# Attention in a decoder trunk: normalising the probabilities, or normalising their product with V

## The chip, the cores and the metric

The kernel runs on one core of a Trainium2 chip. The metric is the device time of one execution in microseconds (us). Before the change it is 1347.07 us, the median of three runs (1344.91, 1347.07, 1347.83).

## What is computed

A two-layer decoder trunk over 512 tokens of width 1024, in float32. Layer AB has a sparse mixer A (8 heads) and a forgetting mixer B (8 heads); layer C has a mixer of 16 heads with three branches: a compressed, a selected and a window branch, each scaled by a learned gate. After each mixer comes an output projection and a squared-ReLU MLP. Cut to what matters here:

```python
def masked_softmax(s, mask):
    s = jnp.where(mask, s.astype(jnp.float32), -jnp.inf)
    m = jnp.max(s, axis=-1, keepdims=True)
    m = jnp.where(jnp.isfinite(m), m, 0.0)
    e = jnp.where(mask, jnp.exp(s - m), 0.0)
    return e / jnp.maximum(jnp.sum(e, axis=-1, keepdims=True), 1e-30)
...
        p = masked_softmax(logits, causal[None, None]).astype(v.dtype)
        return jnp.einsum('bhqs,bshd->bqhd', p, v)
...
        out = gb[..., 0:1] * o_c + gb[..., 1:2] * o_s + gb[..., 2:3] * o_w
```

The division by the sum, and the gate, scale a whole row of `p`, one number for each query and head. So they can be applied to `p`, or to the row of `p @ v`.

## The kernel before

Activations lie feature by token (128 features x 512 tokens, a tile of 256 KB). Dense products take each operand as two fp32r parts, high and low, and three matmuls a product (`mm3`); weights arrive in tiles `raw`, and are split into `whi` and `wlo`. The results stand in PSUM tiles `psd` (`psn`, `psv`, `psva` for some).

The program is written as many small generators, and a planner (`Planner`, L134) puts their instructions in order when the program is built: at each step it takes the instruction that can start first by a table of costs and latencies. So the order on each engine is fixed at build time, and every engine runs its own list in that order. The generators share numbered slots: a generator that asks for a slot (`TU.get`, `PST.get`) waits in a line, first come first served, until one is put back. The profile gives all of these instructions one line, L299 (`group` and `Queue` record them), so its rows are told apart by the names of tiles.

Attention works on pairs of heads. A pair (in layer C, one branch of a pair) is eight units: two heads by four query blocks of 128, with 1 to 4 key blocks (128 to 512 columns). `unit` (L667) does one of them:

1. it takes one of the four SBUF slots `TU` (tile `t`) and one of two PSUM slots `PSS` (`pss`), and TensorE computes the scores;
2. VectorE adds the mask and finds the row's extremum `nm` in one custom instruction; ScalarE takes the exponential, with the row's sum `den` read from its accumulator;
3. VectorE takes the reciprocal `rec` of `den`, 128x1; GpSimd or VectorE, as the planner sees fit, multiplies `t` by `rec` and by the gate (1 in layer AB);
4. TensorE transposes `t` block by block into one of the two PSUM slots `PST` (`ptp`), after which `t` goes back to `TU`, and ScalarE or VectorE copies `ptp` to the pair's tile `pt`.

At most about six units of a pair are under way at once (`WIN`, L40). When all eight are done, `pv` (L689) multiplies `pt` with V into the only slot `PSO` (`po`): the two heads write the two halves of the 128 rows. In layer AB `o_evac` (L696) then splits `po` into `oh` and `ol`, the operands of the output projection. In layer C `pv_c` (L1529) adds three things in the same `po`: the selected branch, the window branch, and the compressed branch (one matmul, `vcb` by `ptc`), and then splits it. `pv_ab` (L1085) and `pv_c` call these.

While attention runs, TensorE also has dense products to do: in layer AB the last input projections and the half of the output projection whose heads are done (`half_out`, L1107); in layer C the query projections `q1` to `q7` of `ORDER_C` (L42) and again `half_out`. Behind the last pair stands `last_out` (L1136), which keeps the product with the last pair's `oh` back until nine other products (27 matmuls) are done.

Of the kernel before, what the change touches and what calls it, by code (L numbers as in the profile page):

```python
# [11 lines left out]
OP = mybir.AluOpType  # L12
# [119 lines left out]


class Planner:  # L134
    """Emits the instructions of many cooperating generators, each in its own order, always the one
    whose operands and engine are ready first; a generator yields an instruction, a choice of
    instructions, a slot it needs or a future it waits for."""

    def __init__(self, tc):
        self.free = {}  # L140
# [177 lines left out]
def trunk(ctx: ExitStack, tc: tile.TileContext, A):  # L318
# [36 lines left out]
    def small(n, name="sm"):  # L355
        return mp.tile([P, n], F32, tag=f"m{n}", name=name)

    def copy(out, src):
        return [SC.activation(out, src, AF.Copy), V.tensor_copy(out, src)]
# [30 lines left out]
    pev = C["pev"].rearrange("p (a b) -> p a b", b=8)  # L390
    w2k, w2v, fold = C["w2k"], C["w2v"], C["fold"]

# [1 line left out]
    jobs = []  # L394
    job_added = [Future()]

# [134 lines left out]
    def futures(n):  # L531
        return [Future() for _ in range(n)]

# [1 line left out]
    class Stats:  # L535
        def __init__(self, rows=P, total=KT, cols=S):
            self.rows, self.total, self.n, self.cols = rows, total, 0, cols
# [112 lines left out]
    def get2(slots, name, dtype=None):  # L650
        return (yield ("all", [slots.get(name, dtype), slots.get(name, dtype)]))

# [1 line left out]
    def scores(ps, qs, kk, qb):  # L654
        n = P * (qb + 1)
        q = qs[:, qb * P:(qb + 1) * P]
# [7 lines left out]
        return bass.AP(tensor=base.tensor, offset=base.offset,  # L664
                       ap=[base.ap[0], [S + P, qb + 1], [1, P]])

    def unit(qs, kk, qb, bias, pt, h, fut, gate=None):  # L667
        n = P * (qb + 1)
        t = yield TU.get("t")
        b = yield from bias(t)  # L670
        ps = yield PSS.get("pss")
        yield scores(ps, qs, kk, qb)
        nm, den, rec = small(1, "nm"), small(1, "den"), small(1, "rec")
        yield V.tensor_tensor_reduce(out=t[:, :n], in0=ps[:, :n], in1=b, op0=OP.add, op1=OP.min,
                                     scale=-0.125, scalar=3e38, accum_out=nm)
        put(PSS, ps)
        yield SC.activation(t[:, :n], t[:, :n], AF.Exp, scale=-1.0, bias=nm, accum_out=den)
        yield V.reciprocal(rec, den)
        g = 1.0 if gate is None else gate
        yield [e.tensor_scalar(t[:, :n], t[:, :n], rec, g, op0=OP.mult, op1=OP.mult) for e in (G, V)]  # L680
        tt = yield PST.get("ptp")
        yield group([T.transpose(tt[:, j * P:(j + 1) * P], t[:, kb * P:(kb + 1) * P], ident)
                     for kb in range(qb + 1) for j in [kb if h == 0 else qb - kb]])
        put(TU, t)
        yield copy(pt_dst(pt, h, qb), tt[:, :n].rearrange("p (a b) -> p a b", b=P))
        put(PST, tt)
        done(fut)
# [5 lines left out]
                                  pt[:, kb, kb * P:S] if h == 0 else pt[:, 4 - kb, 0:m],  # L693
                                  start=first and kb == 0, stop=last and kb == 3) for h in range(2)])

    def o_evac(ps, fut):  # L696
        oh, ol = yield from get2(O, "oh")
        yield copy(oh, ps)
        yield minus(ol, ps, f(oh))
        put(PSO, ps)  # L700
        done(fut, (oh, ol))

# [1 line left out]
    wab = A["wab"]  # L704
    x0 = futures(KT)
    u = futures(KT)
# [351 lines left out]
    def attention_ab():  # L1058
        for kind in ("b", "a"):
            for i in range(4):  # L1060
                q = yield qf[kind, i]
                k = yield kf[kind, i]
                pt = yield PT.get("pt")
                fs = []
                for n_ in range(8):
                    if kind == "b":
                        h, qb = n_ // 4, n_ % 4
                        if qb == 0:
                            yield cumf[2 * i + h]
                            bt = yield B.get("bb")  # L1070
                            yield SY.dma_start(bt, cumd[2 * i + h, :].partition_broadcast(P))
                            bb = [bt, 4]
                        bias = b_bias(bb, P * (qb + 1))
                    else:
                        h, qb = n_ % 2, n_ // 2
                        yield scf[qb]
                        bias = plain_bias(scr[qb])
                    fu = Future()
                    fs.append(fu)
                    spawn(unit(q[h], k[h], qb, bias, pt, h, fu), PR_ATT)  # L1080
                    if len(fs) > WIN:
                        yield fs[-WIN]
                spawn(pv_ab(kind, i, fs, pt, q, k), PR_PV)

    def pv_ab(kind, i, fs, pt, q, k):  # L1085
        for x in fs:
            yield x
        put(Q, *q)
        for x in k:
            put(K, *x)  # L1090
        if kind == "b":
            yield vbf[i // 2]
            v = vb
        else:
            yield vaf
            v = va
        po = yield PSO.get("po")
        yield from pv(po, pt, [[v[kb][:, (2 * i + h) * 64:(2 * i + h) * 64 + 64] for kb in range(4)]
                               for h in range(2)], True, True)
        put(PT, pt)  # L1100
        if i == 3:
            put(O, *v)
        yield from o_evac(po, och[(4 if kind == "b" else 0) + i])


# [1 line left out]
    def half_out(wo, half, och, base, spill, base_ready=None):  # L1107
        fs = futures(KT)
        for m in range(KT):
# [61 lines left out]
    ready = half_out(A["wout0"], 1, och, lambda m: A["xT"][:, m, :], spa)  # L1171
    st1, u1, hT = last_out(A["wout0"], 0, och, spa, ready, 1, "h1")

# [1 line left out]
    def mlp(hT, u, st, w1, w2, after, halves=False):  # L1175
        rnf, rbf = Future(), Future()
        spawn(layer_norm(st, rnf, rbf), PR_ATT)
# [71 lines left out]

    mlp(hT, u1, st1, A["w1"][0], A["w2"][0], after0)  # L1250

# [1 line left out]
    wc = A["wc"]  # L1253
    rnc, rbc, rotc = Future(), Future(), Future()
    spawn(layer_norm(st2, rnc, rbc, rotc), PR_ATT)
# [251 lines left out]
    def attention_c():  # L1507
        for pr in range(8):
            g = pr // 4
            q = yield qsc[pr]  # L1510
            po = Future()
            for bi, br in enumerate(("s", "w")):
                kk = (yield kst[br])[g]
                gat = yield gatf
                pt = yield PT.get("pt")
                fs = []
                for qb in range(4):
                    n = P * (qb + 1)
                    for h in range(2):
                        col = 3 * (2 * pr + h) + 1 + bi  # L1520
                        fu = Future()
                        fs.append(fu)
                        spawn(unit(q[h], kk, qb, plain_bias(cm[:, S - n:S]), pt, h, fu,
                                   gate=gat[:, qb, col:col + 1]), PR_ATT)
                        if len(fs) > WIN:
                            yield fs[-WIN]
                spawn(pv_c(pr, bi, fs, pt, q, po), PR_PV)

    def pv_c(pr, bi, fs, pt, q, pof):  # L1529
        g = pr // 4  # L1530
        for x in fs:
            yield x
        yield vsf
        if bi == 0:
            po = yield PSO.get("po")
        else:
            po = yield pof
        vv = [vsv[kb][:, 128 * bi + 64 * g:128 * bi + 64 * g + 64] for kb in range(4)]
        yield from pv(po, pt, [vv, vv], bi == 0, False)
        put(PT, pt)  # L1540
        if bi == 0:
            done(pof, po)
            return
        ptc = yield ptcf[pr // 2]
        vcb = yield vcf
        yield T.matmul(po, vcb[:, g, pr % 2, :], ptc, start=False, stop=True)
        if pr % 2:
            put(B, ptc)
            put(Q, *((yield qsc[pr - 1]) + q))
# [2 lines left out]
                put(K, *(yield kst[br])[g])  # L1552
        if pr == 7:
            put(O, *gbox["vsw"])
        yield from o_evac(po, occ[pr])

    spc = dram("spc")
    ready = half_out(A["wout1"], 0, occ, lambda m: spb[m], spc, spb_ready)
# [156 lines left out]
```

## Time and profile before

| | |
|---|---|
| median of three runs | 1347.07 us |
| span of the profiled execution, first to last instruction | 1347.5 us |
| TensorE (PE) busy | 1269.8 us, 94% |
| VectorE (DVE) busy | 830.8 us, 62% |
| ScalarE (ACT) busy | 632.3 us, 47% |
| GpSimd (POOL) busy | 450.0 us, 33% |

The profile lists no time around the span. The program stands in this order in the span: layer AB's input projections and attention to about 280 us, its output projection and MLP to about 677, layer C's projections from there, layer C's attention from about 745 to 945, its output projection, and the second MLP to the end. A matmul's row lasts until its result has drained, while the next one has already started; so the time that a matmul costs TensorE is read from the start of one to the start of the next.

### The profile page before, as it was taken

Reading aid. Unit: us, or ns where it says so; the run is one execution under the profiler, and the core shown is the slowest. Engines: PE = TensorE matmul, PEld = TensorE weight load, DVE = VectorE, ACT = ScalarE, POOL = GpSimd, SP = SyncE. Lnnn points to the kernel's source line nnn. Section 1 sums busy time; section 2 is a strip of 40 time slices with the busy share of each in tenths; the row PEclk is TensorE's granted clock in tenths of the full one; section 3 lists DMA queues with packets and bytes.
Section 4 is the critical chain, followed back from the end, with each engine's and each line's share of the span. In section 5 each row is a group of like instructions: output and inputs, shape, how many; then the busy total and the mean of one; then the engine's idle time right before and its main releaser. Section 6 shows DMA issues by size and latency. Waiting matters only on the chain.

```text
span 1347.5 us, 18599 instructions
## 1 busy us (share of the span) xinstructions
PE 1269.8 (94%) x6226; PEld 1011.4 (75%) x6226; DVE 830.8 (62%) x1709; ACT 632.3 (47%) x1331; POOL 450.0 (33%) x428
## 2 busy tenths in 40 slices
PE   6789998997999999999998899999989999999996
PEld 4668766675888888888877566666778888888896
DVE  6999977838434434345677877675644343443475
ACT  4465587742423424334345687776333242342442
POOL 3755887544300000000366656555440000000044
PEclk8899999998999999999997999999989999999998
DMA  6112212153232232232423200013523223232242
GB/s 227 65 55 72 87 63 70 64 193 97 94 99 97 94 101 95 96 100 99 161 66 119 101 24 17 9 35 123 170 74 101 94 98 98 95 102 94 95 155 96
DMA packets 71455, 127.80 MB, mean 95 GB/s; under 512 B 7928, under 2 KB 12536, under 8 KB 71360
## 3 DMA queue, kind: packets, MB, share of 16 engines
q1 hardware_dynamic: 71360, 126.62, 28.5%
q8 instruction: 50, 0.82, 0.3%
q14 instruction: 45, 0.37, 0.1%
HBM read 118.18 MB, written 8.40 MB: 94 GB/s over the span
## 4 chain that ended last, share of the span: by engine, by line
PE 75%; DVE 17%; issue 4%; ACT 2%; POOL 1%; DMA 0%; SPq 0%; POOLq 0%; DVEq 0%; ACTq 0%
PE psd L299 61%; PE po L299 4%; PE ptp L299 3%; PE pss L299 3%; DVE t L299 2%; DVE acc L299 2%; DVE scr L299 1%; DVE m L299 1%; DVE q L299 1%; PE psv L299 1%; DVE ul L299 1%; DVE wlo L299 1%; DVE hT L299 1%; PE pstat L299 1%; DVE whi L299 1%
## 5 line engine op out<-in xcount | busy, mean ns | idle before, releaser
L299 ACT ACTIVATE whi<-raw 128x512 fp32r<-128x512 f32 (+2 forms) x386 | 238.1, 619 | 473.6 <-PE psd L299 447.4
L299 POOL TENSOR_TENSOR wlo<-raw,whi 128x512 fp32r<-128x512 f32 (+1 forms) x143 | 193.2, 1354 | 730.7 <-ACT whi L299 422.7
L299 PE MATMUL psd<-uh,whi 128*128 128x512 f32 x760 | 305.9, 403 | 11.3 <-ACT uh L299 6.3
L299 PE MATMUL psd<-uh,wlo 128*128 128x512 f32 x760 | 301.5, 397 | 1.6 <-POOL wlo L299 1.6
L299 PE MATMUL psd<-ul,whi 128*128 128x512 f32 x760 | 301.3, 396 | 0.0
L299 DVE TENSOR_TENSOR wlo<-raw,whi 128x512 fp32r<-128x512 f32 (+1 forms) x253 | 183.4, 726 | 122.4 <-ACT whi L299 122.1
L299 PE MATMUL psd<-al,whi 128*128 128x512 f32 (+1 forms) x576 | 210.6, 366 | 0.0
L299 PE MATMUL psd<-ah,whi 128*128 128x512 f32 (+1 forms) x576 | 210.6, 366 | 0.0
L299 PE MATMUL psd<-ah,wlo 128*128 128x512 f32 (+1 forms) x576 | 210.5, 365 | 0.0
L299 PEld LDWEIGHTS psd<-uh,whi 128*128 128x128 f32 x760 | 146.3, 193 | 42.5 <-ACT uh L299 6.3
L299 PEld LDWEIGHTS psd<-uh,wlo 128*128 128x128 f32 x760 | 145.5, 191 | 34.3 <-POOL wlo L299 3.2
L299 PEld LDWEIGHTS psd<-ul,whi 128*128 128x128 f32 x760 | 146.1, 192 | 28.5 <-DVE ul L299 0.5
L299 ACT ACTIVATE t<-t,nm 128x128 f32<-128x128 f32 (+2 forms) x192 | 107.2, 559 | 46.0 <-DVE nm L299 43.1
L299 DVE TENSOR_TENSOR hT<-psd,hT 128x512 f32<-128x512 f32 (+1 forms) x88 | 56.3, 641 | 109.8 <-PE psd L299 109.8
L299 PEld LDWEIGHTS psd<-al,whi 128*128 128x128 f32 x576 | 108.6, 189 | 17.6 <-DVE al L299 0.2
L299 PEld LDWEIGHTS psd<-ah,whi 128*128 128x128 f32 x576 | 108.6, 189 | 17.6
L299 PEld LDWEIGHTS psd<-ah,wlo 128*128 128x128 f32 x576 | 108.6, 189 | 17.5
L299 DVE SCALAR_TENSOR_TENSOR t<-psd,rb 128x512 f32<-128x512 f32 x64 | 44.1, 691 | 108.3 <-PE psd L299 108.3
L299 PEld LDWEIGHTS ptp<-call,t 128*128 128x128 f32 x480 | 57.1, 141 | 54.9 <-POOL t L299 17.4
L299 PE MATMUL ptp<-call,t 128*128 128x128 f32 x480 | 83.4, 279 | 13.3 <-DVE t L299 9.5
L299 POOL TENSOR_SCALAR t<-t,rec,gat 128x128 f32<-128x128 f32 (+3 forms) x103 | 65.4, 639 | 64.1 <-DVE rec L299 48.3
L299 ACT ACTIVATE pt<-ptp 128x384 f32<-128x384 f32 (+3 forms) x186 | 77.6, 434 | 19.2 <-PE ptp L299 18.0
(245 smaller groups left out, 1778.7 us busy)
## 6 DMA issues: line engine op xcount, KB each, us to landing
raw<-w SPq DMA_DIRECT2D x272, 256.0 KB, 2.5
raw<-wab SPq DMA_DIRECT2D x38, 256.0 KB, 2.6
raw<-wout SPq DMA_DIRECT2D x32, 256.0 KB, 2.6
raw<-wc SPq DMA_DIRECT2D x24, 256.0 KB, 2.7
raw<-wcn SPq DMA_DIRECT2D x16, 152.0 KB, 2.2
x<-xT SPq DMA_DIRECT2D x8, 256.0 KB, 5.8
raw<-wbv SPq DMA_DIRECT2D x8, 256.0 KB, 2.6
bb<-cumd SPq DMA_DIRECT2D x8, 256.0 KB, 3.6
```

Source lines behind the costliest of these rows:

```text
L299: call = lambda: getattr(self.engine, method)(*args, **kw)
```

## The change

A unit no longer normalises. The sums of a pair's eight units go to the columns of one tile `den` (128x8). When `pv` is done, `scaled` takes the reciprocal of that tile, in layer C multiplies it by the gates, and lets TensorE spread it: for each query block and head one matmul with a column of `rec`, repeated 64 times, as the stationary operand and the identity as the moving one, which leaves in PSUM (`prec`, one of the two `PST` slots) the factor of every query on the 64 rows of its head. The factors are copied to a tile `rs`, one of the four `TU` slots, and VectorE multiplies `po` by them into `rs`. In layer C each branch gets its own `po`; the first branch's scaled result stays in its `TU` slot until the second's is there, one instruction adds the two, the compressed branch's matmul gets a `po` of its own, and one more instruction adds that. `o_split` then splits from SBUF.

```diff
-    def unit(qs, kk, qb, bias, pt, h, fut, gate=None):
+    def unit(qs, kk, qb, bias, pt, h, fut, den):
...
-        nm, den, rec = small(1, "nm"), small(1, "den"), small(1, "rec")
+        nm = small(1, "nm")
...
-        yield SC.activation(t[:, :n], t[:, :n], AF.Exp, scale=-1.0, bias=nm, accum_out=den)
-        yield V.reciprocal(rec, den)
-        g = 1.0 if gate is None else gate
-        yield [e.tensor_scalar(t[:, :n], t[:, :n], rec, g, op0=OP.mult, op1=OP.mult) for e in (G, V)]
+        yield SC.activation(t[:, :n], t[:, :n], AF.Exp, scale=-1.0, bias=nm,
+                            accum_out=den[:, 2 * qb + h:2 * qb + h + 1])
...
-    def o_evac(ps, fut):
+    def dens():
+        return few.tile([P, 8], F32, tag="den", name="den")
+
+    def scaled(ps, den, gate=None):
+
+        rec = few.tile([P, 8], F32, tag="rec", name="rec")
+        yield V.reciprocal(rec, den)
+        if gate is not None:
+            yield V.tensor_tensor(rec.rearrange("p (t h) -> p t h", h=2),
+                                  rec.rearrange("p (t h) -> p t h", h=2), gate, op=OP.mult)
+        pr = yield PST.get("prec")
+        yield group([T.matmul(pr[64 * h:64 * h + 64, t * P:(t + 1) * P],
+                              rec[:, 2 * t + h:2 * t + h + 1].to_broadcast([P, 64]), ident,
+                              start=True, stop=True) for t in range(4) for h in range(2)])
+        rs = yield TU.get("rs")
+        yield copy(rs, pr)
+        put(PST, pr)
+        yield V.tensor_tensor(rs, ps, rs, op=OP.mult)
+        put(PSO, ps)
+        return rs
+
+    def o_split(o, fut):
         oh, ol = yield from get2(O, "oh")
-        yield copy(oh, ps)
-        yield minus(ol, ps, f(oh))
-        put(PSO, ps)
+        yield copy(oh, o)
+        yield minus(ol, o, f(oh))
+        put(TU, o)
         done(fut, (oh, ol))
...
-        yield from o_evac(po, och[(4 if kind == "b" else 0) + i])
+        o = yield from scaled(po, den)
+        yield from o_split(o, och[(4 if kind == "b" else 0) + i])
...
-    def pv_c(pr, bi, fs, pt, q, pof):
+    def pv_c(pr, bi, fs, pt, q, pof, den, gate):
...
+        po = yield PSO.get("po")
+        vv = [vsv[kb][:, 128 * bi + 64 * g:128 * bi + 64 * g + 64] for kb in range(4)]
+        yield from pv(po, pt, [vv, vv], True, True)
+        put(PT, pt)
+        o = yield from scaled(po, den, gate)
         if bi == 0:
-            po = yield PSO.get("po")
-        else:
-            po = yield pof
-        vv = [vsv[kb][:, 128 * bi + 64 * g:128 * bi + 64 * g + 64] for kb in range(4)]
-        yield from pv(po, pt, [vv, vv], bi == 0, False)
-        put(PT, pt)
-        if bi == 0:
-            done(pof, po)
+            done(pof, o)
             return
+        o0 = yield pof
+        yield [e.tensor_tensor(o, o, o0, op=OP.add) for e in (V, G)]
+        put(TU, o0)
         ptc = yield ptcf[pr // 2]
         vcb = yield vcf
-        yield T.matmul(po, vcb[:, g, pr % 2, :], ptc, start=False, stop=True)
+        po = yield PSO.get("po")
+        yield T.matmul(po, vcb[:, g, pr % 2, :], ptc, start=True, stop=True)
...
-        yield from o_evac(po, occ[pr])
+        yield V.tensor_tensor(o, po, o, op=OP.add)
+        put(PSO, po)
+        yield from o_split(o, occ[pr])
```

The planner orders the new instructions, and everything else anew. Two places of that order follow; numbers behind a tile's name tell its instances apart.

The first is TensorE in layer C, late in its attention. Before, in the fifth pair: `pss` are scores, `ptp` transposes (one row a unit), `po` the products with V of the branch before.

```order
L299 MATMUL po_8830<-pt_8778,vsw_6592 64x512 x2
L299 MATMUL ptp_9037<-call_119,t_8957 128x128 x2
L299 MATMUL pss_9046<-ck_6369,cq_8836 128x512
L299 MATMUL pss_9046<-ck_6370,cq_8836 128x512
L299 MATMUL ptp_9042<-call_119,t_8986 128x128 x2
L299 MATMUL pss_9058<-ck_6369,cq_8837 128x512
L299 MATMUL pss_9058<-ck_6370,cq_8837 128x512
L299 MATMUL po_8830<-pt_8778,vsw_6592 64x384 x2
L299 MATMUL ptp_9060<-call_119,t_9014 128x128 x3
L299 MATMUL ptp_9070<-call_119,t_9024 128x128 x3
L299 MATMUL po_8830<-pt_8778,vsw_6593 64x256 x2
L299 MATMUL po_8830<-pt_8778,vsw_6593 64x128 x2
```

Of the change, in the last pair, from the spread `prec_9128` on (it belongs to the branch before; the product with V of that branch stands just ahead of these rows):

```order
L299 MATMUL prec_9128<-call_119,rec_9124 64x128 x8
L299 MATMUL ptp_9147<-call_119,t_9119 128x128
L299 MATMUL pss_9136<-ck_6233,cq_8501 128x256
L299 MATMUL pss_9136<-ck_6234,cq_8501 128x256
L299 MATMUL pss_9151<-ck_6233,cq_8502 128x256
L299 MATMUL pss_9151<-ck_6234,cq_8502 128x256
L299 MATMUL ptp_9159<-call_119,t_9121 128x128
L299 MATMUL pss_9163<-ck_6233,cq_8501 128x384
L299 MATMUL pss_9163<-ck_6234,cq_8501 128x384
L299 MATMUL ptp_9170<-call_119,t_9123 128x128 x2
L299 MATMUL pss_9176<-ck_6233,cq_8502 128x384
L299 MATMUL pss_9176<-ck_6234,cq_8502 128x384
```

Eight matmuls of a spread are new, and the parts of a product with V that stood between the units before do not stand there now.

The second place is ScalarE beside it. Before, in the last pair: exponentials (`t,den<-t,nm`) and copies of transposes to `pt`.

```order
L299 ACTIVATE t_9539,den_9556<-t_9539,nm_9555 128x256
L299 ACTIVATE pt_9441<-ptp_9564 128x128
L299 ACTIVATE t_9546,den_9561<-t_9546,nm_9560 128x256
L299 ACTIVATE pt_9441<-ptp_9570 128x128
L299 ACTIVATE t_9575,den_9590<-t_9575,nm_9589 128x384
L299 ACTIVATE t_9583,den_9598<-t_9583,nm_9597 128x384
L299 ACTIVATE pt_9441<-ptp_9594 128x2x128
L299 ACTIVATE t_9611,den_9617<-t_9611,nm_9616 128x512
L299 ACTIVATE pt_9441<-ptp_9608 128x2x128
L299 ACTIVATE pt_9441<-ptp_9624 128x3x128
```

Of the change, the stretch that answers to the TensorE rows above; `rs_9198<-prec_9128` is the copy that empties the spread's PSUM slot.

```order
L299 ACTIVATE pt_9117<-ptp_9147 128x128
L299 ACTIVATE t_9123,den_9118<-t_9123,nm_9154 128x256
L299 ACTIVATE pt_9117<-ptp_9159 128x128
L299 ACTIVATE t_9150,den_9118<-t_9150,nm_9157 128x256
L299 ACTIVATE t_9162,den_9118<-t_9162,nm_9168 128x384
L299 ACTIVATE t_9175,den_9118<-t_9175,nm_9179 128x384
L299 ACTIVATE pt_9117<-ptp_9182 128x2x128
L299 ACTIVATE t_9186,den_9118<-t_9186,nm_9190 128x512
L299 ACTIVATE pt_9117<-ptp_9194 128x3x128
L299 ACTIVATE rs_9198<-prec_9128 128x512
L299 ACTIVATE pt_9117<-ptp_9201 128x3x128
```

The copy of the spread stands behind the copies of four of the pair's units and five exponentials (a fifth unit's copy, of `ptp_9170`, is on VectorE).

## Rows read from the trace of the kernel before

**Rows 1.** The page: busy time by engine (share of the span), and one group of instructions.

```profile
PE 1269.8 (94%) x6226; PEld 1011.4 (75%) x6226; DVE 830.8 (62%) x1709; ACT 632.3 (47%) x1331; POOL 450.0 (33%) x428
...
L299 DVE TENSOR_TENSOR wlo<-raw,whi 128x512 fp32r<-128x512 f32 (+1 forms) x253 | 183.4, 726 | 122.4 <-ACT whi L299 122.1
```

**Rows 2.** Windows: us, PE, PEld, DVE, ACT, POOL busy (instructions), PEclk, DMA share, GB/s.

```profile
150.00:280.00 130.00, 120.09 (x626) 86.37 (x626) 104.81 (x298) 97.04 (x241) 94.51 (x95) 0.99 0.24 79
...
400.00:425.00 25.00, 25.00 (x112) 20.71 (x111) 9.32 (x15) 6.95 (x11) 0.00 (x0) 1.00 0.31 95
...
745.00:945.00 200.00, 193.13 (x1134) 128.93 (x1135) 144.69 (x500) 148.18 (x433) 115.97 (x144) 1.00 0.14 48
```

**Rows 3.** Waits, 745 to 945 us: who waited for whom, us in total, times, longest.

```profile
POOL t L299 <- DVE rec L299: 48.3, 52, 2.2
...
PEld ptp L299 <- POOL t L299: 14.8, 24, 1.0
...
PE ptp L299 <- DVE t L299: 1.6, 3, 1.2
...
PE ptp L299 <- DVE rec L299: 0.7, 2, 0.5
PE ptp L299 <- POOL t L299: 0.5, 2, 0.3
```

**Rows 4.** Waits, 150 to 280 us.

```profile
PE ptp L299 <- DVE t L299: 6.2, 7, 1.6
...
PEld ptp L299 <- POOL t L299: 2.5, 4, 0.9
...
PE ptp L299 <- DVE rec L299: 0.8, 1, 0.8
PE ptp L299 <- POOL t L299: 0.7, 2, 0.4
```

**Rows 5.** PE timeline: start, us, instruction, count; starts tell what each costs.

```profile
930.71 0.95 PE L299 MATMUL pss<-ck,cq 128*128 128x384 f32 x4
931.59 1.08 PE L299 MATMUL po<-pt,vsw 128*64 128x512 f32 x4
...
941.02 2.37 PE L299 MATMUL po<-pt,vsw 128*64 128x512 f32 x16
```

**Rows 6.** Lines by form, 745 to 945 us: count, busy us, mean ns, idle before.

```profile
L299 PE MATMUL ptp<-call,t 128*128 128x128 f32 x320 | 55.2, 280 | 3.5 <-DVE t L299 1.6 <-DVE rec L299 0.7 <-POOL t L299 0.5
...
L299 ACT ACTIVATION_READ_ACCUMULATOR t<-t,nm 128x1 f32 x128 | 24.2, 189 | 0.0
L299 POOL TENSOR_SCALAR t<-t,rec,gat 128x512 f32<-128x512 f32 x29 | 23.4, 809 | 21.5 <-DVE rec L299 13.3 <-PE pss L299 6.1 <-PE ptp L299 1.9
L299 ACT ACTIVATE t<-t,nm 128x512 f32<-128x512 f32 x32 | 23.0, 719 | 9.4 <-DVE nm L299 9.2
...
L299 DVE RECIPROCAL rec<-den 128x1 f32<-128x1 f32 x128 | 19.9, 158 | 23.7 <-ACT t L299 22.7
...
L299 ACT ACTIVATE pt<-ptp 128x512 f32<-128x512 f32 x32 | 18.7, 594 | 5.3 <-PE ptp L299 5.0
...
L299 ACT ACTIVATE t<-t,nm 128x256 f32<-128x256 f32 x32 | 16.1, 506 | 5.4 <-DVE nm L299 5.1
...
L299 ACT ACTIVATE pt<-ptp 128x256 f32<-128x256 f32 x32 | 11.7, 371 | 1.5 <-PE ptp L299 1.3
...
L299 PE MATMUL po<-pt,vsw 128*64 128x128 f32 x64 | 6.6, 284 | 0.0
...
L299 DVE TENSOR_TENSOR wlo<-raw,whi 128x512 fp32r<-128x512 f32 x6 | 6.1, 1010 | 0.3 <-ACT whi L299 0.3
...
L299 DVE TENSOR_TENSOR oh<-po,oh 128x512 fp32r<-128x512 f32 x7 | 4.8, 680 | 1.0 <-ACT oh L299 1.0
```

**Rows 7.** Windows of PE alone: us, busy (instructions), PEclk, DMA share, GB/s.

```profile
700.00:725.00 25.00, 19.48 (x95) 0.80 0.27 78
...
825.00:850.00 25.00, 24.59 (x150) 1.00 0.05 16
```

More of the change, by code (lines that the diff above doesn't have):

```diff
@@ L1063, in attention_ab @@
                 pt = yield PT.get("pt")
-                fs = []
+                fs, den = [], dens()
                 for n_ in range(8):
@@ L1079, in attention_ab, with pv_ab @@
                     fs.append(fu)
-                    spawn(unit(q[h], k[h], qb, bias, pt, h, fu), PR_ATT)
+                    spawn(unit(q[h], k[h], qb, bias, pt, h, fu, den), PR_ATT)
                     if len(fs) > WIN:
                         yield fs[-WIN]
-                spawn(pv_ab(kind, i, fs, pt, q, k), PR_PV)
-    def pv_ab(kind, i, fs, pt, q, k):
+                spawn(pv_ab(kind, i, fs, pt, q, k, den), PR_PV)
+    def pv_ab(kind, i, fs, pt, q, k, den):
         for x in fs:
@@ L1515, in attention_c @@
                 pt = yield PT.get("pt")
-                fs = []
+                fs, den = [], dens()
                 for qb in range(4):
@@ L1519, in attention_c @@
                     for h in range(2):
-                        col = 3 * (2 * pr + h) + 1 + bi
                         fu = Future()
                         fs.append(fu)
-                        spawn(unit(q[h], kk, qb, plain_bias(cm[:, S - n:S]), pt, h, fu,
-                                   gate=gat[:, qb, col:col + 1]), PR_ATT)
+                        spawn(unit(q[h], kk, qb, plain_bias(cm[:, S - n:S]), pt, h, fu, den), PR_ATT)
                         if len(fs) > WIN:
                             yield fs[-WIN]
-                spawn(pv_c(pr, bi, fs, pt, q, po), PR_PV)
-    def pv_c(pr, bi, fs, pt, q, pof):
+                col = 6 * pr + 1 + bi
+                spawn(pv_c(pr, bi, fs, pt, q, po, den, gat[:, :, col:col + 4:3]), PR_PV)
+    def pv_c(pr, bi, fs, pt, q, pof, den, gate):
         g = pr // 4
```

## The prediction

> **What bounds the kernel now.** Start with the page: TensorE is busy 94% of the span [rows 1], so whatever is added to its work costs time unless a hole takes it. Where the holes are stands in the windows. In the MLPs there are none: 112 matmuls of 512 columns fill 25.00 us, 0.223 us each [rows 2]. The change touches the two attention stretches, 150 to 280 us and 745 to 945 us; there TensorE is busy 120.1 of 130 and 193.1 of 200 us [rows 2]. These rows overstate it, since a row lasts until the matmul has drained, but they rank the engines: ScalarE follows with 148 of 200 us.
>
> Then the waits. In 745 to 945 the first row is GpSimd's multiplication of `t` waiting for the reciprocal, 48.3 us; nobody loses these unless TensorE waits for GpSimd in turn. It does: TensorE's weight loads for transposes waited 14.8 us for GpSimd's `t`, 24 times, its matmuls 1.6, 0.7 and 0.5 us more for VectorE and GpSimd [rows 3]: 17.6 us. In 150 to 280 the same four come to 6.2 + 2.5 + 0.8 + 0.7 = 10.2 us [rows 4]. So 27.8 us of waits end at the step that the change removes. That is the prize, and an upper bound: a late weight load costs only what TensorE does not still spend on older matmuls.
>
> **Removed.** 192 reciprocals of 0.158 us, 138 multiplications on GpSimd (up to 0.81 us) and 54 on VectorE [rows 6]. On their own engines they are free, since neither bounds. What counts is the unit's chain, shorter by a reciprocal, a multiplication and two handoffs. The mean wait for GpSimd was 0.6 us (14.8 over 24 [rows 3]), less than that piece, so each wait could vanish whole. Lower end: only the waits in which TensorE's matmuls themselves stood, 2.8 + 7.7 = 10.5 us [rows 3, 4]; upper end 27.8. I take the middle, **-19 us** (layer AB -7, layer C -12).
>
> VectorE's split of a weight tile, with two operands in SBUF, takes 0.73 us over the program and 1.01 in layer C's attention, where GpSimd is busy 116 of 200 us [rows 1, 2, 6]. The Trainium skill, page "SBUF — State Buffer", section "Who interferes with whom", says that such an instruction and a GpSimd instruction that reads SBUF exclude each other; the two rows agree. By that rule fewer GpSimd instructions give each of those splits 0.28 us back, some 2 us over the six; VectorE has 55 us to spare there, so the sum goes without it.
>
> **Added on TensorE.** 24 spreads of eight matmuls, 64 x 128, float32, in pairs on two halves. The nearest row is a product with V: 16 records in 2.37 us for 1280 columns a half [rows 5], or 1.85 ns a column; a spread has 512 a half: 0.95 us. Upper end: 64 records of the 128-column form cover 6.6 us [rows 6], 0.41 us for each pair of matmuls, four a spread: 1.65 us. I take 0.95, since the spread's matmuls stand back to back like the first row's: **+22.8 us** (AB 7.6, C 15.2; upper end 39.6).
>
> **Added elsewhere.** A spread's copy on ScalarE (0.59 us, the row for 512 columns) and a multiplication on VectorE (0.68 [rows 6]); in layer C an addition from SBUF (about 1.0) and one from PSUM (0.68) a pair; a reciprocal and a gate product on eight columns, below 1 us. No DMA is added or removed; no queue waits for one in these stretches.
>
> What stands last is the tail. From the last pair's spread to its `ol` in layer C: copy 0.59, multiplication 0.68, addition 1.0, addition 0.68, copy 0.59, subtraction 0.7, and six handoffs of about 0.1: 4.8 us, where copy and subtraction took 1.3. In the new order 18 dense matmuls and the compressed product stand between, 4.0 + 0.9 us. I take **+1 us** (0 to 4). In layer AB twelve products of three matmuls more stand there, over 8 us: nothing.
>
> **The new wait.** `scaled` takes a PSUM slot `PST` first and a `TU` slot second. Units of the next branch stand in line for `TU` already, so `rs` comes after them; until then the spread holds one of the two `PST` slots, and transposes get along with one. The order shows it: the spread's copy stands behind four other copies and five exponentials. In layer C it is so in 14 of 16 spreads, with five units' transposes in between; in layer AB in three of eight, with dense work beside them. Layer C's first result also keeps a `TU` slot until the second is there, so units have three.
>
> With one slot, a unit's transposes wait for the copy of the unit before, and that for the exponentials ahead of it on ScalarE. For five units: transposes 5 x 0.28 and four more blocks of about 0.1, 1.8 us; copies 1.8 (0.37 for 256 columns, 0.59 for 512 [rows 6], the others between); ten handoffs 1.0; exponentials of the five units that follow, 0.51 to 0.72 each and 0.19 for the accumulator [rows 6], 3.9. That is 4.6 us if no exponential stands ahead of a copy, 8.5 if each does. I take 6.0, nearer the lower, because VectorE makes some copies. TensorE's own work there is ten score matmuls (2.1 us by columns, four of 384 took 0.88 [rows 5]) and nine blocks, 0.8: 2.9. In seven spans the order has next to no dense matmul, 0.4 us on average: 6.0 - 2.9 - 0.4 = 2.7 us idle each, **+19 us**. The other seven have 3.7 us of dense work, which fills them. Ends: 8 (4.6 us in the sparse ones) and 48 (8.5 in all 14).
>
> **Sum.** 22.8 - 19 + 1 + 19 = +24 us. Against the profiled span of 1347.5, 0.4 above the median of the runs, this gives 1371 us. The ends, 22.8 - 27.8 + 0 + 8 = +3 and 22.8 - 10.5 + 4 + 48 = +64, are not all at one side together; I take 1356 to 1396 as the forecast's own.
>
> **Rivals.**
> - *The slot does not bite.* The planner may have placed the copies where they wait for little, and a spread's copy may run early. Then 22.8 - 19 + 1 = +5: 1352 us. For it: ScalarE has 52 us to spare in layer C [rows 2]. Against it: on an engine that runs its list in order, a copy behind an exponential waits for it.
> - *Faster: the holes take the spread.* All 27.8 us of waits go, and spreads run where TensorE would still stand, in what of 9.9 + 6.9 us of holes [rows 2] is no such wait at a matmul: 16.8 - 10.5, about 6 us. 22.8 - 27.8 - 6 = -11: 1337 us. It decides once a unit's scores are issued early enough for every transpose to find its exponential done. For it: the chain loses its slowest link. Against: with three `TU` slots scores are issued later, not earlier.
> - *The clock falls.* In 700 to 725 us TensorE was busy 19.5 us and its mean granted clock 0.80, which is two fifths of the stretch at the lower of its two levels (1.2 against 2.4 GHz); in 825 to 850, busy 24.6 us, it stayed at 1.00 [rows 7]. If four slices of layer C's attention come to look like the first, each loses some 5 us of work: 1371 + 20 = 1391 us. The Trainium skill, page "TensorE: Matmul & The Clock Gate", section "Part 4: PE-mode transpose", says that transposes do not count as activity for the clock, which speaks against this change: its sparse spans are transposes and a few scores. The second row, a stretch full of transposes at full clock, does not bear that out where other matmuls stand between.
>
> That the instructions move as said needs no rival: the order holds no `TENSOR_SCALAR` on `t` and 24 spreads.
>
> **How the numbers follow.** The forecast gets 0.57, the slot that does not bite 0.20, the faster case 0.13, the clock 0.10. A measurement here tells 0.2%, 2.7 us, from no change. The forecast and the clock are slower throughout; of the second case a quarter comes within 2.7 us. So: faster 0.13, same 0.05, slower 0.82. The range 1345 to 1396 holds the forecast, the second rival and most of the clock, and leaves out the faster case.
>
> **What would show it.** In 745 to 945 us and beyond: waits of transposes for GpSimd gone, waits for `pt` copies and for `t` of ScalarE in their place; layer C's attention longer by about 20 us, layer AB's by 0 to 3; a spread's eight matmuls taking about 0.95 us; copies `rs` several us after their spread; clock 1.00. I am wrong if transposes wait for nothing, or if layer C's attention is shorter than before; and half wrong if it is longer by the 15 us of spreads alone.

## The result, and the profile after

| | before | changed |
|---|---|---|
| median of the runs on one chip | 1347.45 us (4 runs, 1344.91 to 1348.70) | 1387.11 us (4 runs, 1386.04 to 1392.04) |
| ratio, 95% interval | | 1.0300 (1.0280 to 1.0319) |
| span of the profiled execution | 1347.5 us | 1384.3 us |
| mean granted clock of TensorE | 0.976 | 0.977 |

The change costs 40 us. The forecast was 1371 us, slower by 24, in a range of 1345 to 1396: the sign and the place were right, the size was not. The page's first line, to be set against [rows 1]:

```profile
PE 1299.0 (94%) x6610; PEld 1034.4 (75%) x6610; DVE 819.9 (59%) x1557; ACT 638.1 (46%) x1334; POOL 377.9 (27%) x297
```

384 records more on PE are the 24 spreads of 16. Windows of the changed kernel, with the columns of [rows 2]:

```profile
150.00:280.00 130.00, 124.65 (x719) 90.54 (x719) 95.20 (x224) 91.00 (x233) 78.38 (x63) 1.00 0.25 80
400.00:425.00 25.00, 25.00 (x112) 20.72 (x111) 10.05 (x16) 8.22 (x13) 0.00 (x0) 1.00 0.30 95
745.00:990.00 245.00, 222.82 (x1414) 152.17 (x1413) 139.25 (x409) 156.62 (x435) 62.45 (x49) 0.98 0.15 47
```

The loss stands in one place. The last matmul of layer AB's products with V starts at 281.2 us before and at 281.1 us after, and layer C's first scores at 742.8 us (before: 746.4). But the last pair's compressed product (`po<-ptc`), the end of layer C's attention, starts at 990.5 us instead of 943.3: from the first scores to there 247.7 us instead of 196.9. In that stretch TensorE was busy 193 of 200 us before [rows 2] and is busy 223 of 245 now. Part of the longer stretch is dense work of the output projection that came in earlier, so the net loss is less than 51 us.

The waits of 745 to 990 us, to be set against [rows 3]:

```profile
DVE t L299 <- PE pss L299: 50.0, 43, 3.5
...
PEld ptp L299 <- ACT pt L299: 24.8, 28, 1.2
...
PE ptp L299 <- ACT pt L299: 12.9, 21, 1.0
PEld ptp L299 <- ACT t L299: 11.2, 15, 1.3
...
ACT rs L299 <- PE prec L299: 6.0, 2, 5.3
...
PE ptp L299 <- ACT t L299: 1.9, 5, 0.5
...
PE ptp L299 <- DVE pt L299: 1.6, 6, 0.3
```

No transpose waits for GpSimd or for a reciprocal any more. In their place transposes wait for ScalarE's copies of the transposes before them (`pt`) and for its exponentials (`t`): TensorE's matmuls themselves 12.9 + 1.9 + 1.6 us, where it was 2.8 us [rows 3].

One such place in TensorE's timeline of the changed kernel (the spread is `prec`):

```profile
815.60 1.09 PE L299 MATMUL prec<-call,rec 128*64 128x128 f32 x16
816.63 0.33 PE L299 MATMUL ptp<-call,t 128*128 128x128 f32 x1
...
820.36 0.44 PE L299 MATMUL ptp<-call,t 128*128 128x128 f32 x2 [0.52 <-ACT pt L299]
820.56 0.71 PE L299 MATMUL pss<-ck,cq 128*128 128x512 f32 x2
821.98 0.55 PE L299 MATMUL ptp<-call,t 128*128 128x128 f32 x3 [0.71 <-ACT pt L299]
823.39 0.55 PE L299 MATMUL ptp<-call,t 128*128 128x128 f32 x3 [0.87 <-ACT pt L299]
```

and in ScalarE's, where the copy that frees the spread's bank comes:

```profile
822.87 0.47 ACT L299 ACTIVATE pt<-ptp 128x384 f32<-128x384 f32 x1
823.24 0.58 ACT L299 ACTIVATE rs<-prec 128x512 f32<-128x512 f32 x1
823.98 0.49 ACT L299 ACTIVATE pt<-ptp 128x384 f32<-128x384 f32 x1 [0.15 <-PE ptp L299]
```

The spread costs 1.03 us from its start to the next one, and its copy starts 6.6 us after that. Over layer C the copy starts 6.0 to 9.9 us after the start of its spread's last record in 14 of 16 cases, and 0.4 us after it in the last pair's two. Up to here the trace looks as predicted. The experiments ask which of these things costs the time.

### The profile page after: what moved, and what is told of

Same layout as the page of the kernel before. It is cut to its first block, busy times and chain, and to the rows that moved or that the text cites. A ratio compares the mean times of both kernels' runs of the same rounds, so it can differ in the third digit from the quotient of the medians.

```text
span 1384.3 us, 18950 instructions
## 1 busy us (share of the span) xinstructions
PE 1299.0 (94%) x6610; PEld 1034.4 (75%) x6610; DVE 819.9 (59%) x1557; ACT 638.1 (46%) x1334; POOL 377.9 (27%) x297
## 4 chain that ended last, share of the span: by engine, by line
PE 74%; DVE 16%; issue 4%; ACT 3%; POOL 1%; DMA 1%; SPq 0%; POOLq 0%; DVEq 0%; ACTq 0%
PE psd L299 59%; PE po L299 3%; PE pss L299 3%; PE ptp L299 3%; DVE acc L299 2%; PE prec L299 1%; ACT t L299 1%; DVE q L299 1%; DVE scr L299 1%; DVE t L299 1%; DVE m L299 1%; PE psv L299 1%; DVE ul L299 1%; DVE whi L299 1%; DVE hT L299 1%
## 5 line engine op out<-in xcount | busy, mean ns | idle before, releaser
L299 POOL TENSOR_TENSOR wlo<-raw,whi 128x512 fp32r<-128x512 f32 (+2 forms) x144 | 196.8, 1370 | 805.7 <-ACT whi L299 475.5
L299 ACT ACTIVATE t<-t,nm 128x128 f32<-128x128 f32 (+1 forms) x192 | 107.0, 558 | 69.1 <-DVE nm L299 67.7
L299 PE MATMUL ptp<-call,t 128*128 128x128 f32 x480 | 87.3, 284 | 19.3 <-ACT pt L299 12.9
L299 DVE CUSTOM_DVE_ANT_0 t<-pss,call 128x128 f32<-128x128 f32 (+3 forms) x136 | 63.3, 476 | 66.9 <-PE pss L299 53.6
```

The source lines that it names most:

```text
L299: call = lambda: getattr(self.engine, method)(*args, **kw)
```

## The experiments

Every time is a median; the kernel before ran beside each on the same chip (1347.2 to 1347.8 us). With each edit the planner also sets a new order for what stands behind it, so a difference is that of the edit and of its order together.

**1. The scaled results in another pool.** In layer C both scaled results of a pair live in slots of `O` (the pool of 18 for the split outputs) and no longer in `TU`.

```diff
-        rs = yield TU.get("rs")
+        rs = yield (RS or TU).get("rs", F32)
...
-        o = yield from scaled(po, den, gate)
+        o = yield from scaled(po, den, gate, O)
...
-        put(TU, o0)
+        put(O, o0)
...
-        yield from o_split(o, occ[pr])
+        yield from o_split(o, occ[pr], O)
```

> In layer C the two scaled results of a pair live in buffers of the split outputs' pool (18 of them) and no longer in the four TU buffers that the score tiles rotate through; nothing else changes. Theory 1 (slots: the loss beyond the spreads' own work is score tiles and PSUM transposes that wait for a TU buffer or for the PST bank held by a spread): PE's idle in C falls from 46.8 us to near the 26.7 us of the kernel before, total 1387 - 20 = 1367 us (1360 to 1373). Theory 2 (chain: the transposes wait for the exponential and the copies whatever the buffers, the slots only show up as the last of several waits): 1383 us or more. The spread to its copy would be under 2 us by both.

Measured: 1359.17 us, ratio to before 1.0083 (1.0065 to 1.0100). 27.9 us of the 40 go with the slots, more than theory 1 had expected (1360 to 1373 us in all). In layer C every copy of a spread now starts 0.3 to 0.8 us after the start of the spread's last record; layer AB, whose results stay in `TU`, is as it was. The page's first line of this kernel:

```profile
PE 1293.1 (95%) x6610; PEld 1034.3 (76%) x6610; DVE 807.9 (59%) x1543; ACT 636.0 (47%) x1343; POOL 383.8 (28%) x302
```

It has the same 6610 records. The span is 26.0 us shorter (1358.3 against 1384.3): TensorE is not busy for 65.2 us instead of 85.3, which is 20.1 of them, and its rows cover 5.9 us less: where rows overlap, the time counts once, and the closer they stand, the more they overlap. Theory 2 is out.

**2. The buffer before the bank.** The spread asks for its `TU` slot before its `PST` slot.

```diff
+        rs = yield TU.get("rs")
         pr = yield PST.get("prec")
...
-        rs = yield TU.get("rs")
```

> The spread asks for its TU buffer first and only then for the PSUM transpose bank, so that a bank is never held while a spread waits in line for TU; the TU buffers stay as short as in the changed kernel. Theory 1a (it is the held bank, the 'slot jam' as predicted): 1387 - 19 = 1368 us (1362 to 1374). Theory 1b (it is the TU buffers: two of four are lent to scaled results for most of a pair): 1380 us or more, or even slower, as the TU buffer is now held for longer. Theory 2 (chain): no change, 1384 to 1390.

Measured: 1384.00 us, ratio 1.0276 (1.0263 to 1.0290); 3 us back. In layer C the copies start 0.4 to 1.2 us after their spreads, so no bank is held in line, and hardly anything is gained. That speaks for theory 1b, with a limit: the line has only moved ahead of the spread. In 14 of 16 cases the spread now starts 6.1 to 13.2 us after the last matmul of its product with V (0.8 to 3.7 us in the changed kernel), and all that time it keeps `po`, the only `PSO` slot. TensorE's timeline shows what stands in line for it, first a compressed product and then the next branch's product with V:

```profile
872.38 0.66 PE L299 MATMUL ptp<-call,t 128*128 128x128 f32 x4 [0.62 <-ACT rs L299]
873.11 1.13 PE L299 MATMUL po<-ptc,vcb 128*128 128x512 f32 x2
875.01 2.37 PE L299 MATMUL po<-pt,vsw 128*64 128x512 f32 x16 [0.78 <-DVE rs L299]
```

**3. The kernel before with three `TU` slots.** `N_TU = 3` instead of 4.

> The kernel before with three TU buffers in place of four, nothing else: the price of one lent TU buffer alone, in both layers. Theory 1b (TU buffers short): C alone loses 10 us or more, 1357 to 1375 us in all. Theories 1a and 2: TU isn't what bounds, 1347 to 1351 us.

Measured: 1350.49 us, ratio 1.0028 (1.0017 to 1.0040). One slot fewer, all the time, costs 3.3 us there: against theory 1b in its simple form.

**4. Layer C as before.** `unit`, `o_evac`, `attention_c` and `pv_c` of the kernel before for layer C, the changed code for layer AB.

```diff
-                        spawn(unit(q[h], kk, qb, plain_bias(cm[:, S - n:S]), pt, h, fu, den), PR_ATT)
+                        spawn(unit_n(q[h], kk, qb, plain_bias(cm[:, S - n:S]), pt, h, fu,
+                                   gate=gat[:, qb, col:col + 1]), PR_ATT)
```

> Layer AB as in the changed kernel, layer C as in the kernel before. All theories put the loss into C; they differ on what the change is worth in AB: by the prediction's sum (waits -7, spreads +7.6, and two or three jams) 1347 to 1353 us; by the trace of the changed kernel (its first scores of C start 3.6 us earlier than before's) 1343 to 1345 us.

Measured: 1346.13 us (12 runs), ratio 0.9991 (0.9981 to 1.0001). All of the 40 us is layer C's; in layer AB the change is worth nothing that can be told from zero. The time lies between the two that were expected. Three of layer AB's eight copies come 4.8 to 9.4 us after the start of their spread's last record here, as many as the prediction had counted.

**5. Only the first result elsewhere.** Of a pair's two scaled results only the first branch's goes to `O`.

```diff
-        o = yield from scaled(po, den, gate)
+        o = yield from scaled(po, den, gate, None if bi else O)
...
-        put(TU, o0)
+        put(O, o0)
```

> As the run with results elsewhere, but only the first branch's scaled result of a pair leaves the TU buffers; the second branch's result stays in one. The earlier run gave 1359 us against 1387. Theory 1c (the loan that lasts counts: the first result keeps a TU buffer from its copy until the second branch's result is there, some 17 us of each pair's 31): 1359 to 1366 us. Theory 1d (every get counts, because a spread's copy stands in line behind the score tiles, and a pair has two of them): about half comes back, 1370 to 1377 us.

Measured: 1358.76 us, ratio 1.0089 (1.0074 to 1.0105): all of the 28 us come back, as theory 1c had it. Yet the second branch's spread still stands in line with a bank in its hand: its copy starts 5.2 to 5.9 us after the start of the spread's last record in seven pairs of eight, 39 us in sum. So such a jam can cost nothing.

**6. Every spread twice**, in the kernel of experiment 1 (`for _ in range(2)` in the group of matmuls).

> The kernel with C's results elsewhere, and every spread's 16 records on TensorE done twice in both layers (the second time the same values). Theory A (a spread is work on a TensorE that is full): 24 x 0.95 = +22.8 us on 1359, so 1382 (1378 to 1386). Theory B (TensorE's holes take it, C has 24.5 us of them in that kernel): under 1368 us.

Measured: 1390.38 us, ratio 1.0320 (1.0306 to 1.0335); 31.2 us more. Theory A, and more than it: TensorE pays for a spread, it doesn't hide it. The timeline of PE shows the size:

```profile
797.42 1.97 PE L299 MATMUL prec<-call,rec 128*64 128x128 f32 x32
799.32 0.33 PE L299 MATMUL ptp<-call,t 128*128 128x128 f32 x1
```

1.90 us from start to start, 0.95 for each half. Layer C's stretch, first scores to last compressed product, grew by 12.2 us (16 x 0.76). Layer AB's attention, from its first spread to its last, grew by 15.7 us, twice its eight spreads. There a part is the clock; the window of PE in this kernel, then in that of experiment 1 (us, busy, granted clock, DMA share, GB/s):

```profile
200.00:295.00 95.00, 87.16 (x523) 0.93 0.19 62
```

```profile
200.00:295.00 95.00, 93.14 (x539) 1.00 0.30 99
```

A mean of 0.93 over 95 us is 13.3 us at the lower level of the clock, by estimate 6.65 us of work lost. The two windows do not hold the same work, so this is a size and not a proof.

**7. Layer C without its scaling**, in the kernel of experiment 1.

```diff
-        o = yield from scaled(po, den, gate, O)
+        o = yield O.get("rs", F32)
+        yield copy(o, po)
+        put(PSO, po)
```

> The kernel with C's results elsewhere, and in C no reciprocals, spreads and multiplications: the products with V are only copied out of PSUM, so the normalisation and the gates of C's two branches are left out. What then stands between it and the kernel before in C is the shorter chain alone. By the prediction's terms (chain -12, spreads gone): 1347 - 12 = 1335 us (1330 to 1339). By the idle of TensorE in C as read from the first run (24.5 us with the short chain, 27.0 with the long one): 1347 - 2.5 = 1344 us (1341 to 1348).

Measured: 1342.64 us, ratio 0.9964 (0.9950 to 0.9977). Against the kernel of experiment 4, which differs in layer C alone, the shorter chain is worth 1346.13 - 1342.64 = 3.5 us, not 12, with an interval of some 2 us either way. That is net of what came with the change and stays in here: a copy of each product, the sums, and a `po` for each branch. Against experiment 1, the spreads with their reciprocals and multiplications cost 16.5 us.

**8. Layer AB's results in `O` too**, with layer C as before.

> Layer C as in the kernel before, layer AB as in the changed kernel but with its scaled results in the split outputs' pool as well. The version with C as before gave 1346.1. If the jam that the prediction priced at 3 x 2.7 us in AB is there: 1338 us. If AB has TU buffers to lend (its heads are fed by top-k and products, not by the score tiles' turnover): 1345 to 1347 us.

Measured: 1351.38 us, ratio 1.0034 (1.0022 to 1.0046): 5 us slower than experiment 4, and slower than both expectations. Where experiment 4 has three copies 4.8 to 9.4 us late, one is late here, by 3.0 us. So layer AB had jams, and taking them away brought nothing. Why another pool makes it slower was not followed up; the planner then sets another order.

**9. Only the second result elsewhere**, the mirror of experiment 5: `O if bi else None`, and `o_split` returns its slot to `O`.

> The mirror of the run with the first result elsewhere (1359 us): the first branch's scaled result of a pair stays in a TU buffer until the sum, the second's is in the split outputs' pool. Theory 1c' (the first result's loan by itself is the loss): 1380 to 1388 us. Theory 1e (it takes both at once, one buffer lent to the first while the second's spread stands in line for another): 1359 to 1368 us.

Measured: 1367.10 us, ratio 1.0146 (1.0131 to 1.0161). First result elsewhere, 1359; second elsewhere, 1367; neither, 1387. The first result's loan costs 8 us alone and 28 with the second's line behind it. Here the first branch's copies come 4.4 to 7.6 us late in seven pairs of eight, 42 us in sum, about what experiment 5 bore for nothing. That is theory 1e, and it overturns what experiment 5 seemed to say: it is not the long loan by itself.

**10 and 11. Experiment 1 with three, and with two, `TU` slots.**

> C's results elsewhere (1359 us with four TU buffers), and three TU buffers in place of four: the price of one buffer lent all the time, to a chain without the normalisation. If the loss of the changed kernel is a loan of one buffer: C longer by 20 us or more, 1380 to 1390 us. If one buffer is worth what it was in the kernel before (3.3 us): 1360 to 1365 us, and the loss needs two buffers away at once.

Measured: 1362.92 us, ratio 1.0119 (1.0104 to 1.0134): 3.8 us for one slot, the second expectation.

> The same with two TU buffers: two buffers lent all the time. If two away at once make the loss, this must cost more than the whole loss does, as in the changed kernel they are away for part of a pair only: 1359 + 28 or more, 1390 to 1450 us. If it is something else than the number of buffers: under 1385 us.

Measured: 1368.52 us, ratio 1.0162 (1.0145 to 1.0178). Two slots fewer for the whole program cost 9.4 us; the changed kernel lends two for a part of each pair and loses 28. My account by the number of slots fell here: it is something else than their number.

**12. Layer AB without its scaling**, with layer C as before: in `pv_ab` a copy of `po` into a `TU` slot takes the place of `scaled`.

> Layer C as in the kernel before; layer AB without the normalisation: no reciprocals, spreads and multiplications, the products with V are only copied out of PSUM into a TU buffer, so AB's attention output stays unnormalised. The version with AB normalised by spreads gave 1346.1. Difference to it = what 8 spreads cost in AB: 8 x 0.95 = 7.6, so 1338.5, by the prediction's terms (waits removed -7, spreads +7.6); 16 us, so 1330, if a spread costs in AB what the doubling showed there (AB's stretch grew by 15.7 us).

Measured: 1344.62 us, ratio 0.9979 (0.9969 to 0.9989). Both expectations missed: by the difference to experiment 4 the eight spreads cost 1.5 us in layer AB, which its interval of some 2 us does not tell from nothing, and the shorter chain, net of the copies that take its place, brings 2.6 (3.1 against the kernel before on its own chip).

**What fills the waits.** The traces of these kernels, laid side by side, suggest why the same line of waits costs 28 us in one and nothing in another. Layer C's attention has a stock of dense products to put between scores and transposes: the query projections of the later pairs (`psd<-uh` and `psd<-ul`). More comes only from the output projection (`psd<-oh`), whose first half needs the first four pairs. Windows of PE in the changed kernel, all instructions (us, busy, granted clock, DMA share, GB/s):

```profile
780.00:795.00 15.00, 15.00 (x102) 1.00 0.12 36
795.00:810.00 15.00, 14.79 (x97) 1.00 0.11 37
810.00:825.00 15.00, 12.90 (x85) 1.00 0.12 36
825.00:840.00 15.00, 12.74 (x75) 0.89 0.00 1
840.00:855.00 15.00, 13.22 (x88) 1.00 0.05 10
855.00:870.00 15.00, 12.83 (x85) 1.00 0.12 44
870.00:885.00 15.00, 12.31 (x82) 1.00 0.01 2
885.00:900.00 15.00, 12.17 (x80) 1.00 0.00 1
```

and of the `psd` matmuls alone in these windows:

```profile
780.00:795.00 15.00, 7.36 (x27) 1.00 0.12 36
795.00:810.00 15.00, 6.45 (x24) 1.00 0.11 37
810.00:825.00 15.00, 3.66 (x12) 1.00 0.12 36
825.00:840.00 15.00, 0.11 (x1) 0.89 0.00 1
840.00:855.00 15.00, 5.82 (x22) 1.00 0.05 10
855.00:870.00 15.00, 2.44 (x9) 1.00 0.12 44
870.00:885.00 15.00, 0.86 (x3) 1.00 0.01 2
885.00:900.00 15.00, 0.00 (x0) 1.00 0.00 1
```

With 24 or 27 dense matmuls in a window the line of waits can't be seen: TensorE is busy 14.8 and 15.0 of 15 us. With none or three it is busy 12.2 and 12.3. The 22 of 840 to 855 us stand in clumps, and that window is not full either. The kernel of experiment 5, where the second spread jams as before, in the same windows from 855 on:

```profile
855.00:870.00 15.00, 15.00 (x101) 1.00 0.12 37
870.00:885.00 15.00, 15.00 (x103) 1.00 0.06 19
885.00:900.00 15.00, 15.00 (x112) 1.00 0.22 70
```

Its dense matmuls of 860 to 900 us (lines by form, PE):

```profile
L299 PE MATMUL psd<-oh,whi 128*128 128x512 f32 x14 | 4.6, 410 | 0.0
...
L299 PE MATMUL psd<-uh,whi 128*128 128x512 f32 x8 | 3.2, 403 | 0.0
```

and those of the changed kernel, with its transposes:

```profile
L299 PE MATMUL ptp<-call,t 128*128 128x128 f32 x64 | 12.1, 288 | 7.4 <-ACT pt L299 5.1 <-ACT t L299 1.2 <-DVE pt L299 0.8
...
L299 PE MATMUL psd<-oh,whi 128*128 128x512 f32 x2 | 0.6, 396 | 0.0
...
L299 PE MATMUL psd<-oh,wlo 128*128 128x512 f32 x1 | 0.4, 393 | 0.0
```

Few dense matmuls alone do not make a loss, though. Two windows of experiment 1, all of PE:

```profile
810.00:825.00 15.00, 15.00 (x103) 1.00 0.06 19
...
885.00:900.00 15.00, 15.00 (x100) 1.00 0.06 22
```

and the `psd` matmuls alone:

```profile
810.00:825.00 15.00, 2.73 (x9) 1.00 0.06 19
...
885.00:900.00 15.00, 1.71 (x6) 1.00 0.06 22
```

TensorE is full with nine and six of them. There is a second filler: one branch's product with V, of which parts can stand between the next branch's units. Layer C's 16 products stand in 42 pieces in experiment 1 (a piece is a run of `po<-pt` matmuls with no other matmul between) and in 29 in the changed kernel.

Read off the starts in each trace (the fourth pair's compressed product, the last matmul of the stock, the tenth matmul of `oh` with `whi`, by which the output projection has set in), the busy time of PE in 860 to 900 us, and the pieces:

| kernel | time | stock ends | fourth pair | tenth `oh` matmul | PE busy of 40 us | pieces |
|---|---|---|---|---|---|---|
| before | 1347 | 905 | 852 | 912 | 38.7 | 43 |
| 3, before with three `TU` slots | 1350 | 840 | 858 | 864 | 37.6 | 42 |
| 1, results elsewhere | 1359 | 895 | 863 | 919 | 40.0 | 42 |
| 5, first elsewhere | 1359 | 875 | 877 | 889 | 40.0 | 41 |
| 10, three `TU` slots | 1363 | 907 | 876 | 921 | 40.0 | 42 |
| 11, two `TU` slots | 1369 | 867 | 868 | 881 | 39.2 | 47 |
| 9, second elsewhere | 1367 | 858 | 885 | 892 | 36.5 | 33 |
| 2, buffer before bank | 1384 | 855 | 898 | 904 | 34.6 | 22 |
| changed | 1387 | 855 | 897 | 903 | 32.3 | 29 |

Read so, each extra wait is filled from the stock, so a slower pair uses more of it; and it brings the fourth pair later. Where the stock lasts until the fourth pair is done, or nearly (before, 1, 5, 10), waits cost little; where it ends some 18, 28, 43 and 42 us ahead (3, 9, 2, changed) the loss is 3, 8, 25 and 28 us, against the kernel before for the first and experiment 1 for the others. Experiment 11 does not fit: 1 us apart, and 9.4 us lost, of which some 2 us lie ahead of layer C. The pieces tell the costly kernels from the others about as well.

The same repeats at the end: in 945 to 990 us of the changed kernel, with 11, 3 and 10 dense matmuls, PE is busy 13.0, 12.3 and 12.7 of 15 us. The slices from 810 to 900 and from 945 to 990 lack 13.8 + 7.0 = 20.8 us of a busy TensorE, where those of experiment 1 lack 2.2; the two pages differ by 20.1. But 6.1 us of this stand from 810 to 855, before the stock ended: between 819 and 839 us no dense matmul runs, though 24 of the stock are still to come, and why was not asked. So running out of dense work can account for 14.7 us at most. No run here changes the stock alone, or the places of the products with V. Shown is that drawing both results from `TU` costs 27.9 us; by which of these ways stays open.

## Why the prediction was right or wrong

- **Removed, -19 (layer AB -7, layer C -12): wrong in size, in both layers.** The waits for GpSimd did go [rows 3, 4], but they were worth 3.5 us in layer C (experiment 7 against 4) and 2.6 in layer AB (experiment 12). Both are net of the copies, and in layer C the sums, that came instead, which the prediction had priced at nothing. The failing step is "I take the middle" between TensorE's own waits and all waits with those of weight loads. In layer C the lower end, 2.8 us [rows 3], was nearly the answer; the 14.8 us of waiting weight loads were worth little beside it. In layer AB even the lower end, 7.7 us [rows 4], was too much. The split was off as well: the middles of the two layers' own ends are 9 and 10, not 7 and 12.
- **Spreads, +22.8: right in layer C, not in layer AB.** One costs 1.03 us from start to start, 0.95 for each half when doubled; the price of [rows 5] holds. Layer C paid 16.5 us with reciprocals and multiplications, against 15.2. Layer AB paid 1.5, against 7.6, and why so little stays open, since the second set of spreads in experiment 6 cost it 15.7. That layer AB came out near the forecast, -1.1 measured and about +0.6 forecast, is luck: two errors of 4 to 6 us cancel.
- **Tail, +1:** not told apart by any run.
- **The new wait, +19: its form was right, its price was not the bank's alone.** 14 of 16 copies come late in layer C and three of eight in layer AB, as counted in the order, and layer AB's cost nothing that experiment 8 could take away, as forecast. From the end of a spread's matmuls (1.02 us from its start) to its copy the 14 spans are 5.8 to 9.7 us, 7.0 in the mean, where 6.0 was taken; with 7.0 the prediction's own sum gives 7 x 3.7 + 7 x 0.4 = 29 us. That this is near the measured 27.9 does not prove it, for a held bank by itself does not cost it: seven spreads that held one cost nothing in experiment 5, and with all banks given back experiment 2, where the line moved ahead of the spread, won 3 us. What costs is that both results of a pair are drawn from the four slots of the score tiles, 27.9 us (experiment 1). The sparse spans, "In seven spans the order has next to no dense matmul", were read from the order of the changed kernel, so they were in the sum, and 19 us come close to the 20 us of idle in experiment 1's comparison; the rest are 5.9 us that the rows of a sparse TensorE cover more. What was missed is that the spans are no given: with the results in another pool they are gone.
- **The sum.** By experiments 4, 7, 1 and the change itself: -1.1, -3.5, +16.5, +27.9, which is 1347.2 to 1387.1; these are steps from one kernel to the next, so they add up by construction. The forecast's terms, +24, were low mostly by layer C's chain (8.5 us) and by the slots (9). Slips in the prediction's arithmetic did not move the forecast: by its own figures the ends of the new wait are 9 and 50, not 8 and 48, and the faster case is nearer 1336 us than 1337.
- **Rivals.** "The slot does not bite" is what experiment 1 made, and it gave 1359; 1352 was forecast for it. "Faster: the holes take the spread": for layer C experiments 6 and 7 rule it out; in layer AB, where a spread cost 0.2 us by experiment 12, it is near what happened, though not in experiment 6. "The clock falls": mean 0.977 against 0.976; layer C's attention has two slices at 0.89, but the other windows of the sparse stretch from 810 to 900, much of it transposes and scores, are at 1.00. The Trainium skill's page "TensorE: Matmul & The Clock Gate", section "Part 4: PE-mode transpose", says that the fast clock does not engage for transposes. Where scores and other matmuls stand between them, as in 860 to 900 us with 64 transposes at 1.00, these rows don't bear that out; no run here has a long stretch of transposes alone.
- **The side remark on VectorE's splits.** GpSimd is busy 62 of 245 us instead of 116 of 200, and the split did not become faster (745 to 945 us, to be set against [rows 6]):

```profile
L299 DVE TENSOR_TENSOR wlo<-raw,whi 128x512 fp32r<-128x512 f32 x3 | 3.2, 1054 | 0.9 <-ACT whi L299 0.8
```

By the rule of the Trainium skill's page "SBUF — State Buffer", section "Who interferes with whom", as the prediction used it, some of the 0.28 us should have come back. These rows do not show it; three instructions are few, and nothing hung on it.

No version beats both kernels: layer AB changed and layer C as before is the fastest that computes the same, 0.9991 with 1.0001 inside its interval.

## What to carry to other kernels

A weight load that waits is not a TensorE that waits: price a removed wait by the matmul rows rather than by those of weight loads, and with a margin of some us even then (2.8 us of matmul waits brought 3.5 in layer C, 7.7 brought 2.6 in layer AB). A result that lives long should not be drawn from a small pool that a pipeline turns over: moving it to a pool with room gave back 28 of 40 us. Where other work covers the waits, ask what that work is, when it ends and when the next of it starts: the same late copies, some 40 us in sum, cost nothing in one kernel and came with 8 us in another. That the end of such work is what makes the loss was read from traces here, and not shown by an edit.

## What was not expected

Costs in this kernel don't add: the two loans cost 0 us (second alone), 8 us (first alone) and 28 us together. A score tile's pipeline runs with two slots almost as with four (9.4 us over the whole program). And eight spreads that cost 1.5 us in layer AB cost 16 us more when each was done twice, some 6.65 of them by estimate in a clock that fell to a mean of 0.93.
